# Experts as a pipeline of pairs, their weights in contiguous runs, and right-hand pools at multiples of 128 bytes

## The chip, the cores and the metric

The kernel runs on one core of one Trainium2 chip. The metric is the device time of one execution in microseconds (us); less is better. Three executions of the kernel before gave a median of 3131.39 us.

## The reference, cut to what matters

Two transformer blocks of two layers each work on 512 tokens of width 1024, in fp32. A layer of the first block has a mixer (two kinds of attention side by side), an attention to 256 memory tokens, and 16 experts that choose their tokens. The second block has four groups of 256 columns (Fourier, neighbourhood attention, spatial gate, differential attention) and a feed-forward network (FFN) of width 4096, both modulated by a condition vector (the "ada" parameters).

```python
for l in range(2):                                   # first block
    x = x + parallel_mixer(rms_norm(x, ln_mix[l]), w_in[l], ...)
    x = x + memory_cross_attention(rms_norm(x, ln_mem[l]), rms_norm(mem, ln_mem_kv[l]), ...)
    x = x + expert_choice_moe(rms_norm(x, ln_ffn[l]), w_router[l], w_gate[l], w_up[l], w_down[l])

def expert_choice_moe(h, w_router, w_gate, w_up, w_down):
    affinity = softmax(h @ w_router)                 # 512 tokens x 16 experts
    gate, idx = top_k(affinity.T, 64)                # each expert takes its 64 best tokens
    x_in = h[idx]                                    # 16 x 64 x 1024
    a, u = x_in @ w_gate, x_in @ w_up                # 16 x 64 x 512
    y = (silu(a) * u) @ w_down * gate                # 16 x 64 x 1024
    return zeros(512, 1024).at[idx].add(y)
```

## The kernel before

**Layout.** The residual `x` lies transposed in eight tiles `x0` to `x7` of 128 x 512 (features by tokens). Products that need full precision are made of three products of halves: `split` (L358 to L366) writes a high half `H` with ScalarE and a low half `L` with VectorE, and `mm3` (L345 to L356) multiplies high by high (L353), high by low (L354) and low by high (L356). Weights of this kind come in slabs of 1 MiB: a raw tile `wr` of 128 x 2048 is loaded, and `wsplit` makes of each half of it a pair `wh`, `wl` of 128 x 1024 (L334 on ScalarE, L335 on VectorE). In the FFNs these pairs take turns with pairs `vh`, `vl` from another pool. TensorE holds a 128 x 128 piece of them and moves 512 columns of `h` past it.

**Experts.** `experts` (L871) goes through 4 groups of 4 experts. For a group it gathers the chosen tokens with 72 products of a one-hot matrix `oh` (L888), for both pairs of the group at once (tiles `xin`). Then it takes each pair of experts. Per expert, gate and up are 8 matmuls each (L930) with 64 rows of output; gate fills columns 0 to 63 of the array and up columns 64 to 127. ScalarE moves the result to `au` (L933), TensorE transposes it (L936), ScalarE takes silu (L938) and VectorE the product (L939), which gives `gg`. Down (L948) makes the width of 1024 in two halves of 8 matmuls each per pair; here the pair's first expert (h = 0) fills the lower 64 columns, the second (h = 1) the upper. `split` with the gate makes `yy` of it (L365, L366), and 16 matmuls with the transposed one-hot matrix `ohT` (L956) scatter it, whose results VectorE adds to `x` (L957). A matmul of L930 or L948 is two instructions in the profile.

**Weights.** An expert's weights are 6 tiles `we` of 1 MiB (two each for gate, up, down), loaded by SyncE's queue (L288) in program order into a ring of 14 buffers in layer 0 and 12 in layer 1 (`NWE`). A load waits until the last matmul has read the tile that had its buffer before. Each of a tile's 128 partitions gets 4 runs of 2 KB from memory.

**Order.** The Tile framework's scheduler orders each engine's instructions from its own estimate of times; a tile's buffer is given out in program order, and the pools of a stage are put on either side of the memory (`side="right"`), so that a tile of one stage may have to wait for a tile of the stage before that lies at the same place. In `run` (L1675), the raw and split weights of mixer and memory attention (`WTS2`, the pool `wa0` or `wa1`) lie on the right side, as does the ring of `we`.

Of the kernel before, what the change touches and what calls it, by code (L numbers as in the profile page):

```python
# [248 lines left out]
class Kernel:  # L249
# [622 lines left out]
    def experts(k, l, routed):  # L872
# [2 lines left out]
        for g in range(4):
            oh = []
            for t in range(4):
                o = k.t("oh", (128, 4, 64), F32R)
                nc.vector.tensor_tensor(o, slots, slot[:, t, 4 * g:4 * g + 4].unsqueeze(2).to_broadcast([128, 4, 64]),
                                        op=OP.is_equal)  # L880
                oh.append(o.rearrange("p e s -> p (e s)"))
            xin = [k.t("xin", (128, NK, 128)) for _ in range(2)]
            for c in range(NK + 1):
                p = k.ps("mm")
                for t in range(4):
                    for j in range(2):
                        w = T[t][j][:, c * 128:c * 128 + 128] if c < NK else (aH, aL)[j][:, t, :]
                        nc.tensor.matmul(p[:w.shape[1], :256], w, oh[t], start=(t == 0 and j == 0), stop=(t == 3 and j == 1))  # L888
                if c < NK:
                    gain = k.gain(("ln_ffn", l), c)  # L890
                    nc.vector.tensor_scalar(xin[0][:, c], p[:, :128], gain, None, op0=OP.mult)
                    nc.scalar.activation(xin[1][:, c], p[:, 128:256], AF.Copy, scale=gain)
                else:
                    ga = k.t("ga", (17, 256))
                    nc.vector.tensor_copy(ga, p[:17, :256])
            gates, roots, ohT = [], [], []
            for pr in range(2):
                p = k.ps("T")
                nc.tensor.transpose(p[:, :17], ga[:, pr * 128:pr * 128 + 128], k.ident[:17, :17])
                gt = k.t("s1", (128, 1))  # L900
                for h in range(2):
                    a = slice(64 * h, 64 * h + 64)
                    e = 4 * g + 2 * pr + h
                    nc.vector.tensor_copy(gt[a], p[a, e:e + 1])
                    r = k.t("s1", (128, 1))
                    for b in (slice(0, 64), slice(64, 128)):
                        nc.vector.tensor_copy(r[b], p[a, 16:17])
                    roots.append(r)
                gates.append(gt)
                p = k.ps("T")  # L910
                for t in range(4):
                    nc.tensor.transpose(p[:, t * 128:(t + 1) * 128],
                                        oh[t][:, pr * 128:pr * 128 + 128].bitcast(F32), k.ident)
# [814 lines left out]
```

## Time and profile before

| | |
|---|---|
| Median of three executions | 3131.39 us (3127.49 to 3134.98) |
| The profiled execution, its own time | 3128.5 us |
| Its span in the profile | 3126.7 us |
| TensorE (PE) busy | 2971.6 us, 95% |
| VectorE (DVE) busy | 1581.2 us, 51% |
| ScalarE (ACT) busy | 1205.4 us, 39% |
| Experts of layer 0, first L930 to last L956 | 474.56 to 742.2 us |
| Experts of layer 1, the same | 1203.62 to 1477.69 us |

The span leaves out 1.8 us around the program. PE's busy time counts overlapping instructions once; a start-to-start difference of neighbouring rows of one engine is the better measure of pace, since the ends of matmuls are modelled.

### The profile page before, as it was taken

To read this page: it belongs to the slowest core of one execution; us is meant where nothing else is said; L and a number is where in the kernel's file an instruction comes from. 1 tells how busy PE (TensorE), PEld (TensorE's weight loads), DVE (VectorE), ACT (ScalarE), POOL (GpSimd) and SP (SyncE) were. 2 spreads that over 40 slices of the span, in tenths; PEclk is the share of its full clock that TensorE was granted. 3 is DMA by queue.
4 is the path that set the end of the run, shared out by engine and by line. 5 is a ranking of instruction groups with operands and counts; after the bars stand their busy time and mean duration, and the time that the engine had idled before them with its cause. 6 is when DMAs were issued, how large, how long until landed. Compare 5 with 4: busy or idle time off the path is not lost.

```text
span 3126.7 us, 42254 instructions
## 1 busy us (share of the span) xinstructions
PE 2971.6 (95%) x16816; PEld 2241.4 (72%) x16816; DVE 1581.2 (51%) x3071; ACT 1205.4 (39%) x2356; POOL 280.7 (9%) x281
## 2 busy tenths in 40 slices
PE   8999979998999988999998899999999998999998
PEld 5677764444666864444887778888888787878887
DVE  5666652224576644234537666334344547654444
ACT  4646431113565532113426554222222336542332
POOL 2111120001102101001300011000000100010000
PEclk9999989999999998999999899999999998999999
DMA  5423249994433228996222311111111222222221
GB/s 183 135 95 122 95 180 332 358 370 172 161 109 115 82 78 316 367 370 242 62 74 70 90 41 55 68 55 68 68 54 54 97 96 71 65 81 95 94 98 64
DMA packets 168756, 422.34 MB, mean 135 GB/s; under 512 B 12144, under 2 KB 21616, under 8 KB 152816
## 3 DMA queue, kind: packets, MB, share of 16 engines
q1 hardware_dynamic: 167536, 416.76, 37.9%
q0 software_dynamic: 1024, 2.89, 0.4%
q8 instruction: 133, 2.18, 0.3%
q14 instruction: 63, 0.52, 0.0%
HBM read 405.18 MB, written 2.10 MB: 130 GB/s over the span
## 4 chain that ended last, share of the span: by engine, by line
PE 89%; DVE 4%; ACT 3%; issue 1%; DMA 1%; POOL 0%; SPq 0%; POOLq 0%; ACTq 0%; DVEq 0%
PE pmm L354 12%; PE pmm L353 12%; PE pmm L356 12%; PE pmm L930 8%; PE pS L353 5%; PE pS L356 4%; PE pS L354 4%; PE pmm L948 4%; PE pT L458 4%; PE pO L704 3%; PE pmm L888 2%; PE pA L998 2%; PE pmm L956 2%; PE pT L492 2%; PE pT L394 1%
## 5 line engine op out<-in xcount | busy, mean ns | idle before, releaser
L334 ACT ACTIVATE wh<-wr 128x1024 fp32r<-128x1024 f32 (+1 forms) x195 | 202.3, 1038 | 533.7 <-PE pmm L354 364.9
L335 DVE TENSOR_TENSOR wl<-wr,wh 128x1024 fp32r<-128x1024 f32 (+1 forms) x195 | 242.0, 1244 | 279.4 <-ACT wh L334 279.0
L930 PE MATMUL pmm<-we,xin 128*64 128x512 f32 x1024 | 238.1, 596 | 0.0
L353 PE MATMUL pS<-h,wh 128*128 128x512 f32 (+1 forms) x480 | 190.0, 400 | 12.5 <-ACT wh L334 10.2
L1616 DVE SCALAR_TENSOR_TENSOR x<-pmm,ada,x 128x512 f32<-128x512 f32 (+1 forms) x136 | 95.5, 717 | 206.4 <-PE pmm L356 206.3
L354 PE MATMUL pmm<-h,wh 128*128 128x512 f32 (+1 forms) x480 | 186.1, 389 | 2.7 <-DVE h L1036 2.6
L354 PE MATMUL pS<-h,wh 128*128 128x512 f32 (+1 forms) x480 | 185.2, 386 | 3.3 <-DVE h L366 3.3
L356 PE MATMUL pS<-h,wl 128*128 128x512 f32 (+1 forms) x480 | 185.2, 390 | 1.9 <-DVE wl L335 1.9
L356 PE MATMUL pmm<-h,wl 128*128 128x512 f32 (+1 forms) x480 | 184.0, 385 | 0.0
L353 PE MATMUL pmm<-h,wh 128*128 128x512 f32 (+1 forms) x480 | 182.9, 390 | 0.9 <-ACT h L1031 0.9
L334 ACT ACTIVATE vh<-wr 128x1024 fp32r<-128x1024 f32 x68 | 71.8, 1060 | 272.9 <-PE pmm L354 237.3
L930 PEld LDWEIGHTS pmm<-we,xin 128*64 128x64 f32 x1024 | 72.8, 137 | 136.8 <-issue 128.8
L379 POOL TENSOR_TENSOR sq<-sq,sq 128x512 f32<-128x512 f32 (+1 forms) x49 | 61.0, 1245 | 1174.7 <-ACT sq L371 1137.6
L948 PE MATMUL pmm<-we,gg 128*64 128x512 f32 x512 | 143.1, 605 | 15.1 <-DVE gg L939 15.1
L460 ACT ACTIVATE pt<-pT 128x512 f32<-128x512 f32 (+1 forms) x200 | 109.6, 554 | 118.9 <-PE pT L458 118.4
L335 DVE TENSOR_TENSOR vl<-wr,vh 128x1024 fp32r<-128x1024 f32 x68 | 83.7, 1233 | 114.0 <-ACT vh L334 114.0
L353 PE MATMUL pmm<-hid,vh 128*128 128x512 f32 (+1 forms) x400 | 139.3, 348 | 0.0
L439 DVE TENSOR_REDUCE s<-pS 128x1 f32<-128x512 f32 (+1 forms) x200 | 124.2, 622 | 27.8 <-PE pS L356 22.0
L354 PE MATMUL pmm<-hid,wh 128*128 128x512 f32 (+1 forms) x400 | 133.9, 350 | 0.0
L354 PE MATMUL pmm<-hid,vh 128*128 128x512 f32 (+1 forms) x400 | 133.8, 347 | 0.0
L353 PE MATMUL pmm<-hid,wh 128*128 128x512 f32 (+1 forms) x400 | 131.3, 349 | 0.0
L446 ACT ACTIVATE e<-pS,s,rt 128x512 f32<-128x512 f32 (+1 forms) x160 | 117.4, 734 | 17.6 <-DVE s L441 17.2
(443 smaller groups left out, 7179.0 us busy)
## 6 DMA issues: line engine op xcount, KB each, us to landing
we<-in_w_gate_dram SPq DMA_DIRECT2D x64, 1024.0 KB, 11.1
we<-in_w_up_dram SPq DMA_DIRECT2D x64, 1024.0 KB, 10.6
we<-in_w_down_dram SPq DMA_DIRECT2D x64, 1024.0 KB, 13.5
wr<-in_w_ff_dram SPq DMA_DIRECT2D x64, 1024.0 KB, 4.8
wra<-in_ada_w_dram SPq DMA_DIRECT2D x96, 512.0 KB, 4.2
wr<-in_w_in_dram SPq DMA_DIRECT2D x27, 1024.0 KB, 4.8
wr<-in_w_o_dram SPq DMA_DIRECT2D x8, 1024.0 KB, 4.8
wr<-in_w_mkv_dram SPq DMA_DIRECT2D x8, 1024.0 KB, 4.9
```

Of the source, the lines that this page charges most:

```text
L334: k.nc.scalar.activation(H[:, :m], raw[:, a:a + m], AF.Copy)
L335: k.nc.vector.tensor_sub(L[:, :m], raw[:, a:a + m], H[:, :m].bitcast(F32))
L353: mm(p, wH, xH, start=(first and j == 0), stop=False)
L354: mm(p, wH, xL, start=False, stop=False)
L356: mm(p, wL, xH, start=False, stop=(end and j == n - 1))
L439: nc.vector.reduce_max(m, s, axis=AX, negate=True)
L446: nc.scalar.activation(e, s, AF.Exp, bias=m, scale=1.0 if scale is None else scale, accum_out=z)
L458: k.nc.tensor.transpose(p[:, t - a, :], src[:, t * 128:(t + 1) * 128], k.ident)
L460: k.nc.scalar.activation(dst[:, a:b], p[:, :b - a, :], AF.Copy)
L930: nc.tensor.matmul(p[a:a + 64], xin[pr][:, c, s], W[n, c // 4][:, c % 4], start=(c == 0), stop=(c == NK - 1))
L948: nc.tensor.matmul(p[64 * h:64 * h + 64], G[h][:, t, :], WD[half][h][:, t], start=(t == 0), stop=(t == 3))
L1616: nc.vector.scalar_tensor_tensor(x, p, mod[:, 40 + o, j:j + 1], x, op0=OP.mult, op1=OP.add)
```

## The change

Four edits are made together.

1. `experts` is cut in three functions. `gather` makes the one-hot matrices, `xin`, gates and `ohT` of a group; `opened` does gate, up and silu of a pair; `closed` does down, split and scatter. Pair n is opened ahead of the closing of pair n-1. The rings follow: `we` 14 to 13 and 12 to 11, `xin` 2 to 3, `gg` 3 to 4, `ohT` 2 to 3.
2. `w_gate`, `w_up`, `w_down` and the ada weights are laid out on the host in the order of the loads, so that each partition gets one run of 8 KB (experts) or 4 KB (ada).
3. The mixer's pool is cut in two (`MIX`, `MIXO`), `wrt` goes to `HEADS`, and the pool `wa` with `wr`, `wh`, `wl` goes from the right side to the left.
4. A tile of 24 floats (96 bytes), `edge`, is put at the right-hand end. The starts of the right-hand tiles move by 96 bytes. Counted from a multiple of 128 bytes, `we` and `wra` stood at 96 and now stand at 0; the second block's `wh`, `wl` at 96, now 0; the mixer's and memory attention's `wh`, `wl` at 32, now 64 (by edit 3). The FFNs' `vh`, `vl` stay at 64.

```diff
+    for n in ("w_gate", "w_up"):
+        o[n] = np.ascontiguousarray(a[n].reshape(2, 16, 2, 4, 128, 512).transpose(0, 1, 2, 4, 3, 5))
+    o["w_down"] = np.ascontiguousarray(a["w_down"].reshape(2, 16, 4, 128, 2, 512).transpose(0, 1, 4, 3, 2, 5))
+    o["ada_w_2"] = np.ascontiguousarray(a["ada_w_2"].reshape(2, 4, 2, 128, 12, 512).transpose(0, 4, 1, 3, 2, 5))
...
-NWE = (14, 12)
+NWE = (13, 11)
...
-HEADS = {"h": 18, **NORMS}
-MIX = {"f": 4, "e": 3, "pt": 4, "sqm": 3, "lat": 6, "kg": 4, "qk": 12, "kr": 2, "vg": 2, "vm": 1, "wk": 2,
-       "rope1": 1, "rope2": 1, "perm": 1, "wrt": 1}
-ROUTED = {"ht": 8, "ap": 2, "slots": 1, "oh": 4, "ga": 1, "xin": 2}
+HEADS = {"h": 18, **NORMS, "wrt": 1}
+MIX = {"f": 4, "e": 3, "pt": 4, "kg": 4, "qk": 12, "vg": 2}
+MIXO = {"sqm": 3, "lat": 6, "kr": 2, "vm": 1, "wk": 2, "rope1": 1, "rope2": 1, "perm": 1}
+ROUTED = {"ht": 8, "ap": 2, "slots": 1, "oh": 4, "ga": 1, "xin": 3}
-EXP = {"au": 2, "gg": 3, "yy": 3, "ohT": 2}
+EXP = {"au": 2, "gg": 4, "yy": 3, "ohT": 3}
...
+    def opened(k, l, n, xin, roots):
+        nc, G = k.nc, []
+        for h in range(2):
+            W = {(name, kh): k.load("we", k.i[name][l, 2 * n + h, kh], (128, 4, 512))
+                 for name in ("w_gate", "w_up") for kh in range(2)}
...
+            for c in range(NK):
+                for a, name in ((0, "w_gate"), (64, "w_up")):
+                    nc.tensor.matmul(p[a:a + 64], xin[:, c, 64 * h:64 * h + 64], W[name, c // 4][:, c % 4],
+                                     start=(c == 0), stop=(c == NK - 1))
...
+    def closed(k, l, n, G, gate, ohT):
+        nc = k.nc
+        WD = [[k.load("we", k.i["w_down"][l, 2 * n + h, half], (128, 4, 512)) for h in range(2)] for half in range(2)]
...
     def experts(k, l, routed):
+        left = None
         for g in range(4):
+            for pr, (xin, gate, roots, ohT) in enumerate(k.gather(l, g, routed)):
+                G = k.opened(l, 2 * g + pr, xin, roots)
+                if left is not None:
+                    k.closed(l, *left)
+                left = 2 * g + pr, G, gate, ohT
+        k.closed(l, *left)
...
+    ctx.enter_context(k.scope("edge", {"edge": 1}, side="right"))
+    k.nc.gpsimd.memset(k.t("edge", (128, 24)), 0.0)
...
-                k.scope(f"wa{l}", WTS2, side="right"), k.scope(f"heads{l}", HEADS), k.scope(f"mix{l}", MIX):
+                k.scope(f"wa{l}", WTS2), k.scope(f"heads{l}", HEADS), k.scope(f"mix{l}", MIX), k.scope(f"mixo{l}", MIXO):
```

The loops inside `gather`, `opened` and `closed` are those of the old `experts`. Lines move: L930 is L934 in the changed kernel, L936 is L940, L948 is L956, L956 is L963, L365 is L372, L334 is L341.

**TensorE, the first pair of layer 0's experts.** Before, its instructions from the last of gate and up (L930) on; `pT` (L936) are the transposes of the second expert's `au`, and `gg_1208` is what silu makes of them:

```order
L930 MATMUL pmm_1205_4619<-we_1204_4617,xin_1169_4439 64x512
L948 MATMUL pmm_1215_4656<-we_1209_4646,gg_1200_4608 64x512
L948 MATMUL pmm_1216_4667<-we_1211_4650,gg_1200_4608 64x512
L936 MATMUL pT_1207_4638<-c_ident_67,au_1206_4636 128x128 x4
L948 MATMUL pmm_1215_4656<-we_1210_4648,gg_1208_4643 64x512
L948 MATMUL pmm_1215_4656<-we_1209_4646,gg_1200_4608 64x512
```

In the changed kernel, the end of the same pair's down matmuls; the transposes (L940) are those of the next pair's second expert, and both `gg` here belong to the pair being closed:

```order
L956 MATMUL pmm_1233_4746<-we_1228_4729,gg_1201_4617 64x512
L956 MATMUL pmm_1233_4746<-we_1229_4731,gg_1209_4652 64x512
L940 MATMUL pT_1224_4717<-c_ident_67,au_1223_4715 128x128 x4
L956 MATMUL pmm_1233_4746<-we_1228_4729,gg_1201_4617 64x512
L956 MATMUL pmm_1233_4746<-we_1229_4731,gg_1209_4652 64x512
L963 MATMUL pmm_1234_4757<-ohT_1187_4565,yy_1230_4733 128x512
```

The two down matmuls of the first expert that stood alone ahead of the transposes are gone, and what follows the transposes no longer reads their result.

**TensorE, the end of a closing.** Before, the last down matmuls of the same pair (L948) and the scatter behind them (L956), whose first product takes the first half of `yy`:

```order
L948 MATMUL pmm_1216_4667<-we_1211_4650,gg_1200_4608 64x512
L948 MATMUL pmm_1216_4667<-we_1212_4652,gg_1208_4643 64x512
L956 MATMUL pmm_1217_4678<-ohT_1186_4556,yy_1213_4654 128x512
L956 MATMUL pmm_1218_4682<-ohT_1186_4556,yy_1213_4654 128x512
L956 MATMUL pmm_1219_4686<-ohT_1186_4556,yy_1213_4654 128x512
```

In the changed kernel, pair 5 of layer 0, from the end of the down matmuls' first half; `pmm_1478` and on are scatters of the first half of the width, `pmm_1482` and on (L963) need the second half of `yy`:

```order
L956 MATMUL pmm_1476_5840<-we_1471_5832,gg_1409_5548 64x512
L940 MATMUL pT_1468_5822<-c_ident_67,au_1467_5820 128x128 x4
L956 MATMUL pmm_1477_5851<-we_1472_5834,gg_1401_5513 64x512
L963 MATMUL pmm_1478_5862<-ohT_1361_5345,yy_1474_5838 128x512
...
L956 MATMUL pmm_1477_5851<-we_1472_5834,gg_1401_5513 64x512
L956 MATMUL pmm_1477_5851<-we_1473_5836,gg_1409_5548 64x512
L963 MATMUL pmm_1482_5878<-ohT_1361_5345,yy_1474_5838 128x512
L963 MATMUL pmm_1483_5882<-ohT_1361_5345,yy_1474_5838 128x512
```

The first half's scatter has moved in front of the second half's down matmuls, and the second half's scatter stands right behind them. In the changed kernel four pairs of layer 0 (4 to 7) and five of layer 1 (2 to 6) end so; before, only layer 0's last pair did, twice (each half waits for its `yy`), and none of layer 1's.

**ScalarE, from layer 0's experts to layer 1's mixer.** Before, from the last half of `yy` (L365) on; `h` and `sq` begin the mixer's norm, `wh` (L334) are the split halves of its first weights:

```order
L365 ACTIVATE yy_1521_6027<-pmm_1524_6040,s1_1464_5799 128x512
L365 ACTIVATE h_1536_6111<-x0_58,c_gains_66 128x512
L371 ACTIVATE sq_1538_6115<-x0_58 128x512
L371 ACTIVATE sq_1541_6121<-x1_59 128x512
L371 ACTIVATE sq_1544_6127<-x2_60 128x512
L371 ACTIVATE sq_1547_6134<-x3_61 128x512
L365 ACTIVATE h_1539_6117<-x1_59,c_gains_66 128x512
L334 ACTIVATE wh_1562_6168<-wr_1561_6166 128x1024
L334 ACTIVATE wh_1564_6172<-wr_1561_6166 128x1024
L365 ACTIVATE h_1542_6123<-x2_60,c_gains_66 128x512
```

In the changed kernel, from the first half of the last pair's `yy` (L372) on:

```order
L372 ACTIVATE yy_1522_6036<-pmm_1524_6038,s1_1449_5744 128x512
L341 ACTIVATE wh_1563_6180<-wr_1562_6178 128x1024
L341 ACTIVATE wh_1565_6184<-wr_1562_6178 128x1024
L372 ACTIVATE yy_1522_6036<-pmm_1525_6049,s1_1449_5744 128x512
L1006 ACTIVATE condz_2558_9957<-cond_2557_9955 128x8x2
L372 ACTIVATE h_1537_6123<-x0_58,c_gains_66 128x512
L378 ACTIVATE sq_1539_6127<-x0_58 128x512
```

The two splits have moved in front of the last half of `yy`; VectorE's `wl` have moved likewise.

## Rows read from the trace of the kernel before

**Rows 1.** The page: span, and TensorE's busy time, share, instructions.

```profile
span 3126.7 us, 42254 instructions
...
PE 2971.6 (95%) x16816; PEld 2241.4 (72%) x16816; DVE 1581.2 (51%) x3071; ACT 1205.4 (39%) x2356; POOL 280.7 (9%) x281
```

**Rows 2.** Windows: busy us (instructions) by engine, granted clock, DMA share, GB/s.

```profile
500.00:510.00 10.00, 10.00 (x42) 4.64 (x41) 5.53 (x9) 0.69 (x1) 0.00 (x0) 1.00 1.05 386
...
14.00:16.00 2.00, 0.34 (x2) 0.18 (x2) 2.00 (x3) 1.49 (x4) 1.26 (x2) 1.00 1.05 419
20.00:22.00 2.00, 2.00 (x10) 1.81 (x9) 0.00 (x0) 0.00 (x0) 0.00 (x0) 0.50 0.98 403
```

**Rows 3.** Waits of PE, experts of layer 0: us in total, times, longest.

```profile
PE pmm L948 <- DVE gg L939: 7.5, 8, 1.0
```

**Rows 4.** Timeline of PE, gathers of layers 0 and 1.

```profile
603.39 7.93 PE L888 MATMUL pmm<-oh,ht 128*128 128x256 f32 x64
...
671.80 7.94 PE L888 MATMUL pmm<-oh,ht 128*128 128x256 f32 x64
...
1332.46 7.93 PE L888 MATMUL pmm<-oh,ht 128*128 128x256 f32 x64
...
1402.46 7.93 PE L888 MATMUL pmm<-oh,ht 128*128 128x256 f32 x64
```

**Rows 5.** Timeline of PE, one pair of layer 0: start, us, instructions, idle before.

```profile
557.47 0.60 PE L936 MATMUL pT<-c_ident,au 128*128 128x128 f32 x4
558.00 2.36 PE L930 MATMUL pmm<-we,xin 128*64 128x512 f32 x9
559.77 0.59 PE L948 MATMUL pmm<-we,gg 128*64 128x512 f32 x1
...
561.62 0.66 PE L936 MATMUL pT<-c_ident,au 128*128 128x128 f32 x4
563.20 7.08 PE L948 MATMUL pmm<-we,gg 128*64 128x512 f32 x28 [0.93 <-DVE gg L939]
570.22 4.16 PE L956 MATMUL pmm<-ohT,yy 128*128 128x512 f32 x16
```

**Rows 6.** Timeline of PE, end of layer 0's experts and the mixer's start.

```profile
740.05 2.11 PE L956 MATMUL pmm<-ohT,yy 128*128 128x512 f32 x8 [0.78 <-ACT yy L365]
744.30 0.51 PE L353 MATMUL pS<-h,wh 128*128 128x512 f32 x1 [2.14 <-ACT wh L334]
...
747.12 0.79 PE L356 MATMUL pS<-h,wl 128*128 128x512 f32 x1 [1.91 <-DVE wl L335]
```

**Rows 7.** Timeline of PE ahead of the experts of layer 0.

```profile
461.67 0.58 PE L861 MATMUL pT<-c_ident,e 16*128 16x16 f32 x4 [9.29 <-DVE e L857]
```

**Rows 8.** Groups of PE by form, last FFN: busy us, mean ns.

```profile
L354 PE MATMUL pmm<-h,wh 128*128 128x512 f32 x112 | 44.3, 395 | 0.0
...
L354 PE MATMUL pmm<-h,vh 128*128 128x512 f32 x112 | 43.6, 389 | 0.0
...
L354 PE MATMUL pmm<-hid,wh 128*128 128x512 f32 x96 | 37.9, 395 | 0.0
```

**Rows 9.** The same view, mixer and memory attention of layer 0, then layer 1.

```profile
L356 PE MATMUL pS<-h,wl 128*128 128x512 f32 x176 | 71.4, 410 | 0.0
...
L356 PE MATMUL pS<-h,wl 128*128 128x512 f32 x32 | 12.5, 400 | 0.0
...
L356 PE MATMUL pS<-h,wl 128*128 128x512 f32 x113 | 46.2, 409 | 1.9 <-DVE wl L335 1.9
...
L356 PE MATMUL pS<-h,wl 128*128 128x512 f32 x96 | 37.2, 397 | 0.0
```

**Rows 10.** Groups of PE by form, FFN of layer 0.

```profile
L353 PE MATMUL pmm<-hid,wh 128*128 128x512 f32 x126 | 48.2, 394 | 0.0
L353 PE MATMUL pmm<-hid,vh 128*128 128x512 f32 x118 | 46.8, 397 | 0.0
```

**Rows 11.** The page: DMA issues; operation, count, KB each, us to landing.

```profile
we<-in_w_down_dram SPq DMA_DIRECT2D x64, 1024.0 KB, 13.5
```

More of the change, by code (lines that the diff above doesn't have):

```diff
@@ L870, in route, with gather @@
         return slots, slot, (aH, aL), T
[L872 removed]
+    def gather(k, l, g, routed):
         nc = k.nc
         slots, slot, (aH, aL), T = routed
[L875 to L957 removed]
@@ new lines, in gather @@
+        oh = []
+        for t in range(4):
+            o = k.t("oh", (128, 4, 64), F32R)
+            nc.vector.tensor_tensor(o, slots, slot[:, t, 4 * g:4 * g + 4].unsqueeze(2).to_broadcast([128, 4, 64]),
+                                    op=OP.is_equal)
+            oh.append(o.rearrange("p e s -> p (e s)"))
+        xin = [k.t("xin", (128, NK, 128)) for _ in range(2)]
+        for c in range(NK + 1):
+            p = k.ps("mm")
+            for t in range(4):
+                for j in range(2):
+                    w = T[t][j][:, c * 128:c * 128 + 128] if c < NK else (aH, aL)[j][:, t, :]
+                    nc.tensor.matmul(p[:w.shape[1], :256], w, oh[t], start=(t == 0 and j == 0), stop=(t == 3 and j == 1))
+            if c < NK:
+                gain = k.gain(("ln_ffn", l), c)
+                nc.vector.tensor_scalar(xin[0][:, c], p[:, :128], gain, None, op0=OP.mult)
+                nc.scalar.activation(xin[1][:, c], p[:, 128:256], AF.Copy, scale=gain)
+            else:
+                ga = k.t("ga", (17, 256))
+                nc.vector.tensor_copy(ga, p[:17, :256])
@@ new lines, in gather @@
+        out = []
+        for pr in range(2):
+            p = k.ps("T")
+            nc.tensor.transpose(p[:, :17], ga[:, pr * 128:pr * 128 + 128], k.ident[:17, :17])
+            gt, roots = k.t("s1", (128, 1)), []
+            for h in range(2):
+                a = slice(64 * h, 64 * h + 64)
+                e = 4 * g + 2 * pr + h
+                nc.vector.tensor_copy(gt[a], p[a, e:e + 1])
+                r = k.t("s1", (128, 1))
+                for b in (slice(0, 64), slice(64, 128)):
+                    nc.vector.tensor_copy(r[b], p[a, 16:17])
+                roots.append(r)
+            p = k.ps("T")
+            for t in range(4):
+                nc.tensor.transpose(p[:, t * 128:(t + 1) * 128],
+                                    oh[t][:, pr * 128:pr * 128 + 128].bitcast(F32), k.ident)
+            o = k.t("ohT", dt=F32R)
+            nc.scalar.activation(o, p, AF.Copy)
+            out.append((xin[pr], gt, roots, o))
@@ new lines, in closed @@
+    def closed(k, l, n, G, gate, ohT):
+        nc = k.nc
+        WD = [[k.load("we", k.i["w_down"][l, 2 * n + h, half], (128, 4, 512)) for h in range(2)] for half in range(2)]
+        yH, yL = k.t("yy", (128, D), F32R), k.t("yy", (128, D), F32R)
+        for half in range(2):
+            p = k.ps("mm")
+            for t in range(4):
+                for h in range(2):
+                    nc.tensor.matmul(p[64 * h:64 * h + 64], G[h][:, t, :], WD[half][h][:, t], start=(t == 0), stop=(t == 3))
+            s = slice(half * 512, half * 512 + 512)
+            k.split(p, yH[:, s], yL[:, s], scale=gate)
+        for cols in (HALVES if l and n == 7 else (ALL,)):
+            for c in range(NK):
+                p = k.ps("mm")[:, cols]
+                for y in (yH, yL):
+                    nc.tensor.matmul(p, y[:, c * 128:c * 128 + 128], ohT[:, cols], start=(y is yH), stop=(y is yL))
+                nc.vector.tensor_add(k.x[c][:, cols], k.x[c][:, cols], p)
@@ L993, in ada @@
             for h in range(4):
[L994 to L995 removed]
+                w = k.load("wra", k.i["ada_w_2"][l, n, h], (128, 2, 512))
                 for q in range(2):
```

62 lines of the change are left out of this document (15 added, 47 removed).

## The prediction

> **What bounds the kernel now.** I read the page first: TensorE is busy 2971.6 of 3126.7 us, 95% [rows 1]. So the kernel is paced by TensorE nearly everywhere, and an edit is worth what it takes from TensorE's own sequence: waits in it, matmuls that run alone where two could run, and the pace of one matmul. In the experts the DMA is the second candidate: in a window inside layer 0's experts it moves 386 GB/s at a share of 1.05, while PE is busy for the whole window [rows 2]. To tell which of the two ends last, I took PE's waits over layer 0's experts. The large entry is 7.5 us in 8 waits for `gg` [rows 3]; no DMA is named. The timeline of gathers says the same: from gather to gather 68.41 us in layer 0 (603.39 to 671.80), which nothing but PE's sequence sets; in layer 1 one such group took 70.00 (1332.46 to 1402.46) [rows 4]. In that one, some 1.6 us were lost, which I put down to weights, since layer 1 has 12 buffers and layer 0 has 14.
>
> **The waits for `gg`.** In one pair the transposes of `au` that nothing waits behind take 557.47 to 558.00, 0.53 us; those ahead of the down matmuls take 561.62 to 563.20, 1.58 us, with an idle time of 0.93 named for `gg` [rows 5]. The difference, 1.05 us, comes in each of 8 pairs: 8.4 us per layer (7.5 by the view of waits, which I keep as the lower bound). In the new order nothing behind the transposes reads their result before the next pair's gate and up have passed, some 13 us of work. The cover goes only at the end of the stage, where no gate and up are left, and there the last pair has the closing before it as cover. I take 8.4 in each layer.
>
> **Matmuls that run alone.** A matmul of gate, up or down uses half of the array's columns, and two on different halves run at the same time. The 28 instructions from 563.20 to 570.22 are 14 matmuls in 7.02 us, of which 12 go in pairs and 2 are alone [rows 5]: 6 + 2 = 8 slots, 0.88 us a slot, so a matmul without a partner costs 0.44. (Two lone ones ahead of the transposes: 559.77 to 561.62, 1.85 us, near 2 slots.) The order of the whole stage has 30 such matmuls in layer 0 before and 20 after; in layer 1, 28 and 22. That is 4.4 and 2.6 us.
>
> **A new wait.** Where a closing ends with the second half's scatter right behind the second half's down matmuls, PE waits for `yy`: 0.78 us at 740.05 [rows 6]. It stands twice in layer 0 before; the new order has four such ends in layer 0 and five in layer 1. I charge 2 x 0.78 = 1.6 us to layer 0 and 5 x 0.78 = 3.9 to layer 1. What is queued behind them is PE's next gate and up, so the time is on the path. If the closings' other work covers them, they cost nothing; I keep that end.
>
> Layer 0 gives 8.4 + 4.4 - 1.6 = 11.2 us, layer 1 8.4 + 2.6 - 3.9 = 7.1.
>
> **The loads.** A group of 4 experts needs 24 tiles, 25.2 MB: 65.2 us at 386 GB/s, of the 68.41 that PE takes. After the sum above layer 0's group takes 65.6 us, of which the gather's 8.8 use no weights. So if 2 KB runs stayed at 386, PE would use 24 tiles in 56.8 us while 65.2 are needed to load them, a lag of 8.4 us per group, made up from the buffers and during the next gather. With 8 KB runs the nearest rows are the first slabs of the mixer, 419 and 403 GB/s at shares of 1.05 and 0.98 [rows 2], mixed with smaller loads; they give 60.1 to 62.4 us, a lag of 3.3 to 5.6. In layer 1 before, the lag was 65.2 - 59.6 = 5.6 us with 12 buffers and cost 1.6 us in one group. With 11 buffers (one tile less, 2.6 us) and a lag of 3.3 to 5.6, I expect that 1.6 to stay about as it is: 0. In layer 0, with 13, nothing. An earlier start of the first tiles is worth nothing: ahead of the first group PE waits 9.29 us for the routing's `e` on VectorE [rows 7], not for a load.
>
> By the Trainium skill ("DMA: Bandwidth & Descriptors", section "Why small descriptors are slow (HBM only)"), each packet carries a fixed overhead of about 3 cycles beside one cycle per 32 bytes. An estimate from that page: 67 cycles per 2 KB against 259 per 8 KB, 3.4% faster, 399 GB/s from the 386; the rows at 403 and 419 lie above it.
>
> **From the experts to layer 1's mixer.** After layer 0's last scatter (740.05, 2.11 us) PE waits 2.14 us for `wh` and then 1.91 for `wl` [rows 6]. The raw slab was loaded late and ScalarE split it behind five pieces of the norm. In the new order both splits stand ahead of the last `yy`, on engines that wait there for PE. Both waits gone would be 4.05 us; but the `h` halves that VectorE makes for the same matmuls set a pace of their own. I take 3, with 0 and 4.05 as ends. The second `wr`, ada and rope loads move a few places on SP's queue; PE does not wait for them now, and I charge nothing (their ends are inside the same 3).
>
> **The pace of a slab.** In the last FFN, matmuls with `wh` (start at 96 past a multiple of 128 bytes) take 395 ns and those with `vh` (at 64) 389, of the same form; with `hid` as the moving side it is 395 too [rows 8]. With neighbouring rows one such matmul after the other, 6 ns each is time on the path. The change puts `wh`, `wl` at 0 there and at 64 (from 32) in the mixers. I found no row for 0 or 32 alone; the mixers' rows run at 397 to 410 ns, waits and cold stretches included [rows 9], not below the 395. Against it, the FFN of layer 0 has `wh` at the same 96 and shows 394 against 397 [rows 10]: no effect where 512 and 256 columns take turns. So I count only stages with 512 columns at a time: mixers and memory attention 3 x (176 + 32 + 113 + 96) = 1251 matmuls, last FFN 3 x (112 + 96) = 624. 1875 x 6 ns = 11.3 us, of which I take 11; the ends are 0, and 17 if the group projections of the second block (about 960 more) gain too.
>
> The row shows 6 ns between starts at 96 and 64. By the Trainium skill ("SBUF — State Buffer", section "Specifications (TRN2)"), the memory is read in lines of 16 bytes; all these starts are multiples of 16, so by that rule the edit is worth 0 and the time is 3108. The row of the last FFN disagrees with it, that of layer 0's FFN agrees.
>
> Ada loads and the memset of `edge`: 96 loads off the path and one POOL instruction ahead of everything; nothing.
>
> **Sum.** 11.2 + 7.1 + 3 + 11 = 32.3 us, from the profiled execution's own 3128.5: 3096.2. That execution is 2.9 us below the median of the three shown; I forecast 3097.
>
> **Rivals.**
> 1. *The slabs gain nothing.* For it: layer 0's FFN. Against it: the last FFN, whose slabs differ in little but the start. 11 us more than the forecast: 3108.
> 2. *Weights come too late at 13 and 11 buffers because 8 KB runs move no faster.* At 386, layer 1's lag grows from 5.6 to 65.2 - 57.8 = 7.4 us per group, with 2.7 us less in the ring: 4.5 more per group on top of the 1.6, about 18 us in layer 1 and 2 in layer 0: 3117, and at twice that price 3137. Against it: the rows at 403 and 419.
> 3. *Slower than before: starvation in every pair.* A closing's 4 tiles now queue behind the 8 of the next pair, so 12 tiles have to pass through 11 or 13 buffers for each pair. If each of 16 pairs waits for one tile (13.5 us from issue to landing in the queue [rows 11], 2.7 us apart at 386), that is 43 us: 3139. It decides from 32.3 / 16 = 2.0 us per pair on. Against it: tiles of gate and up free as each half is done, and with 12 buffers only 1.6 us were lost in a group. By the Trainium skill ("DMA: Bandwidth & Descriptors", section "Where 436 GB/s comes from"), memory gives a core about 358 GB/s; an estimate from it is 70.3 us per group, 4.7 more than the 65.6, or some 38 us in all: 3134. The window at 386 disagrees.
> 4. *The pipeline's gain returns as waits for `yy` on both halves.* Another 9 x 0.78 = 7 us: 3104.
>
> **Chances.** The forecast's own case 0.50 (3084 to 3102), rival 1 0.20, rival 2 0.12 (0.05 of it near its doubled price), rival 3 0.10, rival 4 0.08. The best ends together (no new waits, 4.05, 17) take 12.8 + 11.0 + 4.05 + 17 = 44.9 us and give 3084; I set the low end at 3080 for what the sum leaves out, and the high end at 3118, past rival 2. Differences within 0.2%, 6.3 us, can hardly be told from none. Slower by more: 0.08 (rival 3 but for 0.02 of it); within it: 0.07 (that 0.02 and rival 2's 0.05); faster: the rest, 0.85.
>
> **What would show it.** Right: from gather to gather 65 to 66 us; no wait of down for `gg`; nine waits for `yy` of 0.8; `wh` and `wl` matmuls of the last FFN at 389; no wait for `wh` at the mixer's start; DMA over 400 GB/s at a share near 1.05 in the experts. Wrong: waits of gate, up or down for DMA of over 2 us per pair; `wh` at 395 still; groups of 68 us or more.

## The result and the profile after

The changed kernel takes 3092.26 us (median of four executions, 3090.25 to 3094.25), against 3131.01 for the kernel before in the same comparison: a ratio of 0.9876, 95% interval 0.9859 to 0.9893. It is 39 us faster; the forecast was 34, with a range that holds the result. The profiled execution's span went from 3126.7 to 3091.0, 35.7 us. The page of the changed kernel, in the rows that answer to [rows 1]:

```profile
span 3091.0 us, 42272 instructions
...
PE 2941.1 (95%) x16816; PEld 2229.2 (72%) x16816; DVE 1580.4 (51%) x3071; ACT 1203.5 (39%) x2356; POOL 283.5 (9%) x282
```

PE is still 95% busy: the busy time fell with the span. To see where, I cut both traces at the same instructions (first gate or up, last scatter, first and last `hid`), and so for every run below:

| Stage | before | after | difference | edge alone | no edge | pipeline alone |
|---|---|---|---|---|---|---|
| start to experts, layer 0 | 474.56 | 467.23 | -7.3 | -2.8 | -6.5 | -2.3 |
| experts, layer 0 | 267.22 | 256.86 | -10.4 | 0.0 | -10.4 | -9.6 |
| to experts, layer 1 | 461.84 | 461.33 | -0.5 | +1.6 | -1.7 | +2.5 |
| experts, layer 1 | 273.86 | 265.72 | -8.1 | -1.7 | -8.1 | -8.7 |
| groups, layer 0 | 445.94 | 447.16 | +1.2 | -3.5 | +2.8 | +2.0 |
| FFN, layer 0 | 504.89 | 502.32 | -2.6 | -2.6 | 0.0 | 0.0 |
| groups, layer 1 | 350.64 | 347.16 | -3.5 | -4.4 | 0.0 | +0.2 |
| FFN, layer 1, to the end | 347.78 | 343.25 | -4.5 | -3.3 | -0.4 | -0.4 |

The last three columns are differences from the kernel before in the runs `e2_edge_alone`, `e1_no_edge` and `e5_pipeline_alone`. The experts and layer 0's FFN repeat to 0.1 us in kernels with the same order, with one exception: layer 1's experts took 273.86 us in this profile of the kernel before, but 272.17 and 272.18 in `e2_edge_alone` and `e4_new_runs_alone`, which have its order. So 1.7 of the 8.1 us there are not the change's ("The long group of layer 1", below, has the cause). The two stretches ahead of the experts and the groups of layer 0 differ by up to 6 us between single profiles of kernels alike there, so that a difference of 2 us in them shows nothing. These differences go with TensorE's granted clock: the start took 466.37 us at a mean clock of 0.96 in `e10` and 472.29 at 0.94 in `e13`, which are alike up to there. The groups of layer 1 vary by up to 2.7 us and the last FFN by up to 1.4 in the same way.

The timeline of gathers, layer 0, which answers to [rows 4]:

```profile
511.06 7.93 PE L895 MATMUL pmm<-oh,ht 128*128 128x256 f32 x64
...
575.63 7.94 PE L895 MATMUL pmm<-oh,ht 128*128 128x256 f32 x64
...
643.08 7.83 PE L895 MATMUL pmm<-oh,ht 128*128 128x256 f32 x64
```

From gather to gather it is now 64.57 and 67.45 us, where it was 68.41. The view of PE's waits from 455 to 735 us, which holds the experts of layer 0 and the first 11 us of the next mixer (the line with `h` is the mixer's) and answers to [rows 3] (first line to last):

```profile
PE pmm L963 <- ACT yy L372: 3.9, 5, 0.8
PE pS L361 <- DVE h L373: 3.1, 3, 1.6
...
PE pT L940 <- ACT au L937: 0.8, 1, 0.8
```

The wait of down for `gg` is gone; the scatter's wait for `yy` is there 5 times. In layer 1 the same view has it 7 times, and one wait of the scatter for `x`:

```profile
PE pmm L963 <- ACT yy L372: 5.4, 7, 0.8
...
PE pmm L963 <- DVE x L964: 1.6, 1, 1.6
```

Before, layer 1's experts had no wait for `yy` from ScalarE and two for `x`:

```profile
PE pmm L956 <- DVE x L957: 3.3, 2, 1.8
```

Two windows inside layer 0's experts, to set beside the first of [rows 2]; the last column is GB/s, the one ahead of it the DMA share:

```profile
500.00:510.00 10.00, 10.00 (x47) 4.48 (x44) 3.29 (x6) 2.05 (x4) 0.00 (x0) 1.00 1.01 420
610.00:620.00 10.00, 10.00 (x45) 4.21 (x44) 5.37 (x9) 0.00 (x0) 0.00 (x0) 1.00 1.01 420
```

420 GB/s at a share of 1.01, where it was 386 at 1.05, and PE is busy throughout in both. The end of layer 0's experts and the mixer's start, which answers to [rows 6]:

```profile
722.36 2.11 PE L963 MATMUL pmm<-ohT,yy 128*128 128x512 f32 x8 [0.78 <-ACT yy L372]
724.31 0.40 PE L360 MATMUL pS<-h,wh 128*128 128x512 f32 x1
...
727.01 0.50 PE L361 MATMUL pS<-h,wh 128*128 128x512 f32 x1 [1.32 <-DVE h L373]
...
732.61 0.50 PE L361 MATMUL pS<-h,wh 128*128 128x512 f32 x1 [1.58 <-DVE h L373]
```

The mixer's first product comes directly after the last scatter, without the 2.14 us of idle time that stood there before, but then PE waits for the low halves of `h` from VectorE, 1.32 and 1.58 us in these rows.

### The profile page after: what moved, and what is told of

The parts are those of the page before. It is cut to its first block, busy times and chain, and to the rows that moved or that the text cites. A ratio compares the mean times of both kernels' runs of the same rounds, so it can differ in the third digit from the quotient of the medians.

```text
span 3091.0 us, 42272 instructions
## 1 busy us (share of the span) xinstructions
PE 2941.1 (95%) x16816; PEld 2229.2 (72%) x16816; DVE 1580.4 (51%) x3071; ACT 1203.5 (39%) x2356; POOL 283.5 (9%) x282
## 4 chain that ended last, share of the span: by engine, by line
PE 88%; DVE 5%; ACT 3%; issue 1%; DMA 1%; POOL 0%; SPq 0%; DVEq 0%; POOLq 0%; ACTq 0%
PE pmm L361 12%; PE pmm L360 12%; PE pmm L363 12%; PE pmm L934 8%; PE pS L360 5%; PE pS L361 4%; PE pS L363 4%; PE pmm L956 4%; PE pT L465 4%; PE pO L711 3%; PE pmm L895 2%; PE pmm L963 2%; PE pA L1015 2%; PE pT L401 2%; PE pT L499 1%; PE pO L499 1%
## 5 line engine op out<-in xcount | busy, mean ns | idle before, releaser
L341 ACT ACTIVATE wh<-wr 128x1024 fp32r<-128x1024 f32 (+1 forms) x195 | 201.9, 1036 | 524.8 <-PE pmm L361 362.2
L934 PE MATMUL pmm<-we,xin 128*64 128x512 f32 x1024 | 239.5, 596 | 0.0
L360 PE MATMUL pS<-h,wh 128*128 128x512 f32 (+1 forms) x480 | 187.5, 395 | 10.3 <-ACT wh L341 8.0
L341 ACT ACTIVATE vh<-wr 128x1024 fp32r<-128x1024 f32 x68 | 71.8, 1060 | 265.7 <-PE pmm L361 225.4
L934 PEld LDWEIGHTS pmm<-we,xin 128*64 128x64 f32 x1024 | 73.4, 137 | 137.9 <-issue 132.1
L956 PE MATMUL pmm<-we,gg 128*64 128x512 f32 x512 | 134.0, 597 | 0.0
```

Of the source, the lines that this page charges most:

```text
L341: k.nc.scalar.activation(H[:, :m], raw[:, a:a + m], AF.Copy)
L360: mm(p, wH, xH, start=(first and j == 0), stop=False)
L934: nc.tensor.matmul(p[a:a + 64], xin[:, c, 64 * h:64 * h + 64], W[name, c // 4][:, c % 4], start=(c == 0), stop=(c == NK - 1))
L956: nc.tensor.matmul(p[64 * h:64 * h + 64], G[h][:, t, :], WD[half][h][:, t], start=(t == 0), stop=(t == 3))
```

## The experiments

Twelve kernels were run. Each one's order on all engines is that of the kernel it starts from, but for `e5`, `e6`, `e11` and `e12`. Diffs show the lines that matter; "..." stands for lines left out.

**The right-hand start taken back.** `edge` is left out of the changed kernel.

```diff
-    ctx.enter_context(k.scope("edge", {"edge": 1}, side="right"))
-    k.nc.gpsimd.memset(k.t("edge", (128, 24)), 0.0)
```

> The changed kernel without the tile of 96 bytes: we, wra and the second block's wh, wl start again 96 bytes past a multiple of 128, the mixer's stay at 64; every engine's order is that of the changed kernel. Theory A (the start address of the stationary weights sets TensorE's pace): wh and wl matmuls of the last FFN back at 395 ns, the last FFN longer by 3.7 us, the FFN of layer 0 by about 2.5, the groups by some 1 to 2: 3099 to 3101. Rival B (the FFNs gained through something else, such as DMA traffic): 3092 within 2 us and 389 to 394 ns. If the start also slows the loads, the experts' DMA falls from 420 GB/s toward 386; by A it stays at 420.

Measured: 3103.32 us, ratio to before 0.9918 (0.9901 to 0.9936), 11 us more than the changed kernel. The table has the place: layer 0's FFN, layer 1's groups and the last FFN are back at the times of before to 0.4 us, the experts stay at 256.86. The loads stay at 420 GB/s. Theory A holds, with more than the 7 to 9 us that it gave; 10.3 us of the profile's difference lie in these three stages.

**The right-hand start alone.** The same two lines put into the kernel before.

> The kernel before with the tile of 96 bytes alone; order unchanged. All right-hand tiles move by 96 bytes: the mixer's wh, wl from 32 to 64, the second block's from 96 to 0. Theory A: the gain that the changed kernel shows outside the experts, without the part of the moved pool: mixer and memory attention of layer 0 3 to 7 us, of layer 1 2 to 4, FFNs 6, groups 2: 3113 to 3118. Rival B: 3131 within 2 us.

Measured: 3110.83 us, 0.9941 (0.9926 to 0.9955). 24 floats that nothing reads give half of the whole gain, 2 us more than theory A's range. The profile has 16.7 us of it. 10.3 lie in layer 0's FFN, layer 1's groups and the last FFN, the stages that lose 10.3 us in `e1`; the 1.7 in layer 1's experts are the clock's, and the 3.5 in layer 0's groups and what the mixers show lie within what these stretches vary by. Layer 0's experts keep their 267.25 us.

**The weights in old runs.** The changed kernel with `w_gate`, `w_up`, `w_down` passed as they come, and the loads cut as before:

```diff
...
-            W = {(name, kh): k.load("we", k.i[name][l, 2 * n + h, kh], (128, 4, 512))
+            W = {(name, kh): k.load("we", k.i[name][l, 2 * n + h, kh * 512:kh * 512 + 512].rearrange("(c p) f -> p c f", p=128), (128, 4, 512))
...
-        WD = [[k.load("we", k.i["w_down"][l, 2 * n + h, half], (128, 4, 512)) for h in range(2)] for half in range(2)]
+        WD = [[k.load("we", k.i["w_down"][l, 2 * n + h, :, half * 512:half * 512 + 512].rearrange("(c p) f -> p c f", p=128), (128, 4, 512)) for h in range(2)] for half in range(2)]
```

> The changed kernel with the experts' weights in the old layout, 4 runs of 2 KB per partition; order unchanged. Theory A (the pipeline with 13 and 11 buffers needs the faster loads): 386 GB/s in the experts, PE waits for weights 2 to 7 us in layer 0 and 9 to 18 in layer 1: 3103 to 3117. Rival B (the buffers cover it): 386 GB/s and waits under 2 us: 3092 to 3095.

Measured: 3097.46 us, 0.9897 (0.9883 to 0.9912), which overlaps the changed kernel's interval; the profile's span is 3092.5. Two windows, and the gathers, of its trace:

```profile
480.00:490.00 10.00, 10.00 (x52) 3.69 (x50) 1.85 (x5) 3.64 (x5) 0.00 (x0) 1.00 1.04 385
610.00:620.00 10.00, 10.00 (x44) 4.66 (x42) 6.47 (x11) 1.08 (x2) 0.00 (x0) 1.00 1.05 387
```

```profile
515.20 7.94 PE L894 MATMUL pmm<-oh,ht 128*128 128x256 f32 x64
...
579.77 7.93 PE L894 MATMUL pmm<-oh,ht 128*128 128x256 f32 x64
...
647.20 7.83 PE L894 MATMUL pmm<-oh,ht 128*128 128x256 f32 x64
```

At 387 GB/s the groups take the same 64.57 and 67.43 us, and the experts 256.85 and 265.71, no wait for DMA among PE's waits. By the experts it is rival B: the buffers cover it. The total lies between the two theories' ranges; in the profile the 1.5 us more than the changed kernel come with 4.1 us more ahead of layer 0's experts, a stretch that varies by more.

**The new runs alone.** The kernel before with the experts' weights in runs of 8 KB.

> The kernel before with the experts' weights in contiguous runs of 8 KB alone; order unchanged. Theory A (before the change the loads ended ahead of PE): over 410 GB/s, groups of layer 0 still 68.4 us, the 1.6 us of layer 1's long group gone: 3129 to 3131, no change that can be told. Rival B (the experts were bound by DMA): groups of 64 us or less, 3100 to 3115.

Measured: 3128.9 us, 0.9997 (0.9988 to 1.0007). A gather to the next, and a window at the start of the stage:

```profile
601.42 7.94 PE L891 MATMUL pmm<-oh,ht 128*128 128x256 f32 x64
...
669.84 7.94 PE L891 MATMUL pmm<-oh,ht 128*128 128x256 f32 x64
```

```profile
480.00:490.00 10.00, 10.00 (x48) 3.67 (x45) 2.68 (x11) 3.49 (x6) 0.00 (x0) 1.00 1.00 416
```

416 GB/s, and a group of 68.42 us as before. Theory A.

**The pipeline alone.** The kernel before with `gather`, `opened`, `closed` and their rings (13 and 11 for `we`). The ada weights keep their runs of 4 KB here, as they do in every kernel with the pipeline: that part of edit 2 was never tried by itself.

> The kernel before with the experts as a pipeline of pairs and its rings (13 and 11 buffers) alone: weights in 2 KB runs, mixer pools and right-hand starts as before. Theory A (the pipeline is worth what PE's order says): experts of layer 0 shorter by 10 to 11 us, of layer 1 by 8, nothing elsewhere: 3110 to 3114. Rival B (at 386 GB/s and without the freed places the first tiles come later, and PE waits for them): 2 to 6 us of waits for DMA at the start of each stage, 3115 to 3122.

Measured: 3112.02 us, 0.9946 (0.9931 to 0.996). The experts take 257.64 and 265.12 us: 9.6 less in layer 0, and in layer 1 8.7 less than this profile of the kernel before, 7.1 less than `e2` and `e4`. A window inside layer 0's experts:

```profile
620.00:630.00 10.00, 9.99 (x48) 3.38 (x46) 0.83 (x2) 1.07 (x2) 0.00 (x0) 1.00 1.05 387
```

The DMA runs at its 387 GB/s through this window, and no wait of PE for DMA is named in either layer's experts. Behind the experts it waits for the mixer's weights as before the change:

```profile
PE pS L360 <- ACT wh L341: 2.3, 1, 2.3
PE pS L363 <- DVE wl L342: 1.3, 1, 1.3
```

Theory A.

**The mixer's pools taken back.** The changed kernel with `wa` on the right and one pool `MIX`.

```diff
...
-                k.scope(f"wa{l}", WTS2), k.scope(f"heads{l}", HEADS), k.scope(f"mix{l}", MIX), k.scope(f"mixo{l}", MIXO):
+                k.scope(f"wa{l}", WTS2, side="right"), k.scope(f"heads{l}", HEADS), k.scope(f"mix{l}", MIX):
```

> The changed kernel with the mixer's pools as before (wr, wh, wl on the right, one pool for the rest), pipeline, layout and the tile of 96 bytes kept. wh and wl of mixers then start at 64 past a multiple of 128, but at 201536 instead of 53696. Theory A (only the start within 128 bytes counts, and the pool's move saves the wait from experts to mixer): mixers as in the changed kernel but for 1 to 3 us behind layer 0's experts: 3093 to 3096. Rival B (the place counts too: with the tile of 96 bytes alone, the mixers' matmuls went at 232 ns instead of 234, in the changed kernel at 227): 5 ns on 587 matmuls in each layer, 6 us more: 3097 to 3101.

Measured: 3098.26 us, 0.9905 (0.9887 to 0.9923); the span is 3094.4, 3.4 more than the changed kernel's. The total is in rival B's range, but the intervals overlap, so what the pools' move is worth can't be told from the totals ("From the experts to the mixer", below, reads it from one stretch). The median start-to-start time of the mixers' `wh` and `wl` matmuls of 512 columns is 232 ns here, 227 in the changed kernel. So 64 past a multiple of 128 is not all that counts.

**The mixer's start alone.** The changed kernel with 96 bytes ahead of `wa` and 32 behind it.

> The changed kernel with a tile of 96 bytes in front of the mixer's wr, wh, wl on the left and one of 32 bytes behind them: wh and wl start at 53792, 32 past a multiple of 128, everything else stays where it was or moves by 128; order unchanged. Theory A (the start within 128 bytes counts): mixers' matmuls from 227 back to 233 or 234 ns, 7 us over both layers: 3098 to 3100. Rival B (the place low in memory counts, not the start): 227 ns and 3092 within 2.

Measured: 3094.9 us, 0.9889 (0.9873 to 0.9904). The matmuls go at 234 ns, as theory A has it, but the total is 3 us short of its range and the stages do not show the 7 us: 468.94 and 459.46 us, inside what single profiles of kernels alike there differ by. (`h` moved by 128 bytes here, so its start and that of `wh`, `wl` are not told apart.) How much of the slower pace the whole mixer passes on can't be read from this; over its first 88 us in layer 1 it is 1.1 us (below).

**The second block's start, three values.** The right-hand tile is made larger.

```diff
-    k.nc.gpsimd.memset(k.t("edge", (128, 24)), 0.0)
+    k.nc.gpsimd.memset(k.t("edge", (128, 40)), 0.0)      # e9; in e13 (128, 72)
```

> The changed kernel with a right-hand tile of 160 instead of 96 bytes: the second block's wh and wl start at 212800, 64 past a multiple of 128, instead of 212864 (0); order unchanged. Theory A (64 is as good as 0 or better): 229 ns or less in FFNs and groups: 3090 to 3093. Rival B (64 is good only low in memory: vh at 64 goes at 227 in the last FFN, where it lies at 165312, and at 233 in the FFN of layer 0, at 181696): 232 or 233 ns, 3 to 4 ns on some 2300 matmuls: 3098 to 3101.

> The changed kernel with a right-hand tile of 288 instead of 96 bytes: the second block's wh and wl start at 212672, which is 64 past a multiple of 128 as in e9_right_start_64 (212800), but 192 past a multiple of 256, as vh and vl, the mixer's wh and wl, and h and hid; order unchanged. Theory A (the start within 256 bytes counts, wherever the tile lies): wh, wl at 227 ns in the last FFN and in layer 1's groups (229 in the changed kernel) and at 233 in layer 0's FFN (229): last FFN 1.5 us shorter, layer 0's 2.5 longer, 3090 to 3095. Rival B (right-hand places are slow at 64 past 128): 232 in all stages as in e9_right_start_64, 3099 to 3104.

Measured: `e9` 3105.08 us, 0.9929 (0.9905 to 0.9952); `e13` 3099.31, 0.9894 (0.9875 to 0.9914). A slab is 48 matmuls of the last FFN; its time is the start of the next slab less its own. The timelines of PE below show where such slabs begin. Before the change, one with `wh`, `wl` in the last FFN and the slab of `vh`, `vl` behind it:

```profile
2889.38 0.39 PE L353 MATMUL pmm<-h,wh 128*128 128x512 f32 x1
...
2900.58 0.39 PE L353 MATMUL pmm<-h,vh 128*128 128x512 f32 x1
```

In the changed kernel, first a slab of layer 0's FFN (96 matmuls), then one with `wh`, `wl` and one with `vh`, `vl` of the last FFN:

```profile
2132.87 0.40 PE L360 MATMUL pmm<-h,wh 128*128 128x512 f32 x1
...
2149.53 0.40 PE L360 MATMUL pmm<-h,vh 128*128 128x512 f32 x1
...
2900.83 0.39 PE L360 MATMUL pmm<-h,wh 128*128 128x512 f32 x1
...
2911.82 0.39 PE L360 MATMUL pmm<-h,vh 128*128 128x512 f32 x1
...
2922.70 0.39 PE L360 MATMUL pmm<-hid,wh 128*128 128x512 f32 x1
```

Of `e9`, then of `e13`:

```profile
2908.43 0.40 PE L360 MATMUL pmm<-h,wh 128*128 128x512 f32 x1
...
2919.58 0.39 PE L360 MATMUL pmm<-h,vh 128*128 128x512 f32 x1
```

```profile
2908.59 0.39 PE L360 MATMUL pmm<-h,wh 128*128 128x512 f32 x1
...
2919.47 0.39 PE L360 MATMUL pmm<-h,vh 128*128 128x512 f32 x1
```

In the last FFN a slab takes 10.99 us at 212864 (`vh`: 10.88), 11.15 at 212800, 10.88 at 212672; before the change it took 11.20 at 212960. The seven slabs of a kind with `h` in one trace agree to 0.01 us. In layer 0's FFN one takes 16.66 us in the changed kernel, 16.87 in `e9`, 16.85 in `e13`, 16.82 before. In pace, `e13` is theory A in all three stages: 192 past a multiple of 256 is the best of the starts tried for the last FFN and layer 1's groups, and a bad one for layer 0's FFN, where 128 is the best. In time it is not: layer 0's FFN takes 2.7 us more, as forecast, but the last FFN takes only 0.2 less instead of 1.5 (its mean granted clock is 0.98 instead of 0.99), and the total lies at the low end of rival B's range, with 5.1 us more ahead of layer 0's experts, where single profiles vary. `e9` is rival B in pace, with a total above its range.

**The FFNs' `vh`, `vl` placed low.** They get a scope of their own ahead of `hid`.

```diff
-FFN = {"vh": 2, "vl": 2, "hid512": 16, "hid256": 16}
+FFNV, FFN = {"vh": 2, "vl": 2}, {"hid512": 16, "hid256": 16}
...
-                with k.scope(f"pf{l}", P_GEMM, PSUM), k.scope(f"ffn{l}", FFN):
+                with k.scope(f"pf{l}", P_GEMM, PSUM), k.scope(f"ffv{l}", FFNV), k.scope(f"ffn{l}", FFN):
```

> The changed kernel with the FFNs' vh and vl placed ahead of hid: they start at 132544 instead of 181696 (layer 0) and 165312 (layer 1), all 64 past a multiple of 128, and hid moves up behind them; order unchanged. Theory A (a start at 64 is good low in memory only, with the border near 182000): vh and vl of layer 0's FFN from 233 to 227 ns, 720 matmuls, 4.3 us, layer 1 unchanged: 3087 to 3090. Rival B (the 233 of layer 0 comes from its stage, which alternates 512 and 256 columns, not from the place): 233 ns, 3092 within 2. If the place of hid, the moving side, counts, both FFNs would slow.

Measured: 3093.57 us, 0.9887 (0.9869 to 0.9904). `vh` stays at 233 ns in layer 0's FFN (502.32 us, to the hundredth that of the changed kernel): rival B. The place of `vh` does not count, which left the start within 256 bytes (`e13` tries it).

**The second block's `wh`, `wl` on the left too.**

```diff
-                k.scope("ws", PARTS, side="right"):
+                k.scope("ws", PARTS):
```

> e10_vh_low with the second block's wh, wl on the left too (132544, 64 past a multiple of 128, vh behind them at 148928). The scheduler changes the order at 14 places, all behind layer 1's experts. Theory A (low and 64 gives 227 ns): FFNs' wh, wl from 229 to 227 and vh, vl as in e10_vh_low, 3 us more: 3084 to 3088, less what the start of the second block loses by waiting for tiles of the experts at the same place, 0 to 5 us. Rival B: 229 stays, 3088 to 3095.

Measured: 3103.6 us, 0.991 (0.9895 to 0.9925), slower than either theory had it. 132544 is 192 past a multiple of 256, and the FFNs do as in `e13`: 505.04 us in layer 0's, 227 ns in the last. The groups of layer 0 take 453.05 us, 5.9 more than in the changed kernel, among the stages that vary; the order at the block's start was another one, and what of it is due to that was not tried apart.

**No scatter right behind its down matmuls.** The down weights of the pair to be closed are loaded between the two experts of the pair that is opened (on top of `e10`).

```diff
...
         for h in range(2):
+            if h and left is not None:
+                left = left + (k.down(l, left[0]),)
             W = {(name, kh): k.load("we", ...)
...
```

> e10_vh_low with the down weights of the pair to be closed loaded between the two experts of the pair that is opened. In the order no scatter stands right behind its half's down matmuls any more; there are 6 more lone matmuls in layer 0 and 4 more in layer 1. Theory A (the waits for yy are gone): 3.9 - 2.6 = 1.3 us in layer 0 and 5.4 - 1.8 = 3.6 in layer 1 shorter than in the changed kernel: 255.6 and 262.1 us; 3082 to 3087. Rival B (other waits come in their place, or PE waits for weights as the ring holds the down tiles longer): experts no shorter, 3087 to 3095.

Measured: 3086.38 us, 0.9856 (0.9841 to 0.9871), the fastest of all. Its experts take 252.51 and 261.91 us, 4.4 and 3.8 less than the changed kernel's. The gathers, and PE's waits over layer 0's experts:

```profile
516.75 7.93 PE L895 MATMUL pmm<-oh,ht 128*128 128x256 f32 x64
...
581.09 7.83 PE L895 MATMUL pmm<-oh,ht 128*128 128x256 f32 x64
...
646.50 7.83 PE L895 MATMUL pmm<-oh,ht 128*128 128x256 f32 x64
```

```profile
PE pT L942 <- ACT au L939: 1.7, 2, 0.9
PE pmm L895 <- DVE oh L886: 0.9, 1, 0.9
```

`yy` is not among layer 0's waits. The groups are 64.34 and 65.41 us. The total is theory A's; its sum is not. In layer 0 the stage falls by more than the 3.9 us of waits for `yy`, and in layer 1 other waits come in part in their place, as rival B had it (for `x` 3.8 us instead of 1.6, for `au` 2.6 instead of 1.6), yet the stage falls by 3.8. One reason is the count of lone matmuls: in the traces 22 and 24 start by themselves, against 20 and 22 in the changed kernel, two more per layer instead of 6 and 4. The rest was not found. Against the changed kernel the intervals of the totals still overlap; the 8.2 us are those of the stages.

## Why the prediction was right, point by point

**The waits for `gg`**: right. 8.4 us were forecast for each layer; the views had 7.5 and 7.6 and have none left, and `e5` shows the experts' gain with the pipeline alone (9.6 and 7.1 us).

**Lone matmuls and the new wait**: right in direction; that the sum fits, 18.3 us forecast and 18.5 between the profiles, is luck. 1.7 us of the 18.5 are the clock's in the kernel before (next point): against `e2` and `e4`, layer 1 gains 6.5 us and both layers 16.8. Inside that, two errors work against each other. The wait for `yy` comes 5 and 7 times (3.9 and 5.4 us) instead of 4 and 5: an end of the first half that comes directly behind its down matmuls waits as well, and I had counted only those of the second. In layer 1 I left out a gain of 1.7, the shorter waits for `x` (3.3 to 1.6). The groups of 65 to 66 us that I named as a sign did not come: two of layer 0's five waits for `yy`, 1.55 us, lie in the second of the two above (64.57 and 67.45).

**The long group of layer 1**: wrong, without harm. I put 1.6 us of one group of 70.00 us [rows 4] down to weights. The place is one run of down matmuls in the kernel before:

```profile
1389.73 8.78 PE L948 MATMUL pmm<-we,gg 128*64 128x512 f32 x30 [0.93 <-DVE gg L939]
```

The same run in `e2_edge_alone`, with the same order, rings and 2 KB loads and behind the same two waits, took 7.08 us:

```profile
1388.56 7.08 PE L948 MATMUL pmm<-we,gg 128*64 128x512 f32 x30 [0.93 <-DVE gg L939]
```

Windows around it in the kernel before, with the granted clock in the third column from the end:

```profile
1384.00:1389.00 5.00, 3.98 (x20) 1.28 (x16) 0.42 (x1) 1.01 (x3) 0.00 (x0) 1.00 1.05 387
1389.00:1394.00 5.00, 4.27 (x12) 1.29 (x14) 0.42 (x1) 0.22 (x1) 0.00 (x0) 0.67 1.05 387
1394.00:1399.00 5.00, 5.00 (x22) 1.79 (x19) 0.75 (x1) 1.14 (x2) 0.00 (x0) 0.99 1.05 387
```

The mean clock was 0.67 over 5 us, so the lower of its two levels (1.2 GHz) for about two thirds of them, behind two waits of 0.82 and 0.93. `e2` has both waits and no such fall, so they alone do not explain it, and why it fell in this execution stays open. No wait for a load is in any of it, and from it I had worked out rival 2 and its 18 us. `e3` has the case itself: 387 GB/s, 13 and 11 buffers, and no wait. So the lag of 8.4 us per group that I had set out costs nothing at 13 buffers; that the ring's content covers it follows from the missing waits and was not followed tile by tile.

**The loads**: right that they are worth nothing (`e4`: 0.9997), and that the rate rises, to 420 GB/s and so by 9%. The estimate of 3.4%, from the fixed overhead per packet that the Trainium skill ("DMA: Bandwidth & Descriptors", section "Why small descriptors are slow (HBM only)") states, was too low: the runs show 386 to 420 GB/s. The Trainium skill ("DMA: Bandwidth & Descriptors", section "Where 436 GB/s comes from") gives a core about 358 GB/s from memory, which an estimate under rival 3 drew on; windows of 386, 387 and 420 GB/s lie above it.

**From the experts to the mixer**: right in direction, mis-sized: 3 us forecast, at most 1.6 measured. Both waits for weights (4.05 us) are gone, but PE waits 3.1 us for `h` from VectorE in their place, the pace that I had named as a limit and not priced. The whole stretch to the next experts varies too much to show the rest. Its beginning does not: the first product with `lat` comes 88.4 to 88.5 us after the last row of layer 0's scatter in all seven kernels that have the pools on the left, the mixer's start at 192 and the changed kernel's order there. Before the change, in the changed kernel and in `e8` (with its row of the scatter):

```profile
831.15 0.71 PE L353 MATMUL pS<-wh,lat 128*128 128x512 f32 x2
```

```profile
810.72 0.71 PE L360 MATMUL pS<-wh,lat 128*128 128x512 f32 x2
```

```profile
724.08 2.11 PE L963 MATMUL pmm<-ohT,yy 128*128 128x512 f32 x8 [0.78 <-ACT yy L372]
...
813.57 0.71 PE L360 MATMUL pS<-wh,lat 128*128 128x512 f32 x2
```

That is 91.10 us before (740.05 to 831.15), 88.36 after (722.36 to 810.72), and 89.49 in `e8`. Of the 2.7 us, 1.1 are then the mixer's start by `e8`, which leaves at most 1.6 for this term. `e6`, with the pools taken back, is 1.1 us behind the changed kernel at this place, its slower matmuls included. The granted clock changed as well: over the first 20 us behind the last scatter its mean was 0.83 before and in `e2` and `e4`, 0.75 and 0.74 in `e5` and `e6`, where PE had waited for the split weights, and 1.00 in the changed kernel and the other six.

**The pace of a slab**: the mechanism was right, its parts were mis-sized. The last FFN, forecast 3.7, gave 4.2 (`e1` against the changed kernel) or 3.3 (`e2` against before); 14 whole slabs at 0.20 us each make 2.8 of it. Its `wh` stand at 392 to 394 ns instead of the 389 that I named as a sign, since 128 is not the best start. Layer 0's FFN, forecast 0 by [rows 10], gave 2.6. The groups of layer 1, which stood only in the upper end of 17, gave 3.5 (`e1`) or 1.9 (`e4` less `e2`). The mixers, forecast 7.5, gave about 2 us per layer (means over the 8 profiles with 227 ns and the 6 others: 469.1 against 471.3, and 460.9 against 463.1), no more than they vary, and five of the 6 others also have the pools on the right. The step that failed in [rows 10] is that `vh` was the yardstick: in layer 0's FFN `vh` at 192 is itself slow, so equal times did not mean that the start is without effect. Rival 1, by which the slabs gain nothing, was wrong: the start alone takes the total from 3131.24 to 3110.83 us (`e2`), and its lack costs 11 (`e1`). Some 10 of the 20 us are placed in stages that repeat; the rest lies in those that vary. The Trainium skill ("SBUF — State Buffer", section "Specifications (TRN2)") states lines of 16 bytes; by these alone starts that are all multiples of 32 would not differ, and slabs of 10.88 to 11.20 us disagree.

## What to carry to other kernels

Cost an edit to a PE-bound stage by PE's own order (waits behind transposes, matmuls without a partner, a consumer right behind its producer): that gave 18.3 us for the experts, where 16.8 are the change's, while the transfer rate, 9% better, gave nothing. Where long runs of matmuls set the time, try the start of the stationary tiles in steps of 32 or 64 bytes over 256, stage by stage: it costs a dummy tile. Before a lone slow stretch is put down to a resource, look at the granted clock of that stretch, and at a second profile of the same order. Where the time of a whole stage varies by more than the effect, look for a part of it that repeats.

## What was not expected of the hardware

The pace of 128 x 128 by 512 fp32 matmuls depends on where the stationary tile starts within 256 bytes. Medians of start-to-start times of neighbouring ones:

| start past a multiple of 256 | last FFN | FFN of layer 0 | mixers |
|---|---|---|---|
| 192 | 227 ns (`vh` in all; `wh` in `e13`, `e11`) | 233 | 227 |
| 128 | 229 (`wh`, changed kernel) | 229 | not tried |
| 64 | 232 (`e9`) | 232 | 232 (`e2`, `e6`) |
| 224, 160 or 32 | 232 (224, before) | 233 (224) | 234 (160, before; 32, `e8`) |

The place in memory does not show: starts at 53696, 165312 and 212672, all 192 past a multiple of 256, go at 227 ns. Nor is the period 512: the first two are 448 past a multiple of 512, the third 192. `h` and `hid` started at 192 past a multiple of 256 in all of these but `e8`. Whether the start counts by itself or against that of the moving side was not tried, nor why layer 0's FFN, which takes 512 and 256 columns in turn, has another best start; 0 was not tried either.
